# One token-major section of 512 columns in place of two of 256, for the HGRN values and the gMLP's gated half

## The chip, the cores and the metric

The kernel runs on one core of one Trainium2 chip. The metric is the device time of one execution in microseconds (us). A core has a matrix engine (PE, or TensorE), a vector engine (DVE), a scalar engine (ACT), a general engine (POOL), and SP, which here issues DMAs. Products go to eight PSUM banks of 512 float32 columns. PE holds one operand still (the stationary tile, loaded by a weight load, PEld) and moves the columns of the other through it.

## The reference, cut to what matters

One layer of a diffusion backbone on T = 640 tokens: 512 of the sample and 128 of the prompt, each with D = 1024 features. A normalised and modulated h goes through one wide product, whose columns are thirteen sections of 256, and four token mixers use them: a short convolution, a bidirectional HGRN recurrence, a neighbourhood attention and a gMLP. Then follow gates, an output product and a convolutional feed-forward part.

```python
proj = h @ lw['w_in']
(a_x, a_b, a_c, b_q, b_ff, b_fb, b_i, b_g, c_q, c_k, c_v, d_u, d_v) = jnp.split(proj, IN_SPLITS, axis=-1)
...
y_b, s_f, s_b = hgrn2_bidir(b_q, b_ff, b_fb, b_i, b_g, lb_f, lb_b, lw['hgrn_norm_g'], s0_f, s0_b)
...
y_d = chunk_gmlp(d_u, d_v, lw['gmlp_norm_g'], lw['gmlp_ws'], lw['gmlp_b'])
```

The change concerns `b_i`, the values of the recurrence, and `d_v`, the half of the gMLP that is normalised over its 256 features, mixed over 128 tokens and multiplied by `d_u`. All is float32.

## The kernel before, in words

**Products.** To keep float32's accuracy each operand is split into a high part of fewer bits and the low remainder, and a product is three matmuls: high by high, high by low, low by high. The input h lies in SBUF as feature tiles (`xhk`, `xlk`: 128 features by 640 tokens, high and low). A weight arrives by a DMA of 512 KB that SP issues; ACT copies the high part (L311, L324) and DVE subtracts for the low one (L312, L325).

**The input sections.** `SECTIONS` lists the order in which the columns of `w_in` are made. Eleven of the thirteen are *feature-major*: 128 features of the weight are stationary and the tokens move, in two halves of 320 columns (`gemm_half`, L363); a section is two such tiles, each with a weight load of its own. The other two, `i` and `dv`, are *token-major* (`tok_tile`, L917 on): 128 tokens of h are stationary, and the section's 256 weight columns move (L935). For each of the five token tiles there is one accumulation over 8 feature tiles. The weight comes in two steps (`kh`) of 4 feature tiles, and five PSUM banks hold the five sums across both steps. At the second step each token tile is copied out by ACT (L939): the values into the second half of a region HE (tag E), the gated half into DX1 (tag X1). For `dv` ACT also squares it and sums along the row into `dss` (L941), for the normalisation. A `dv` section takes two PSUM pairs of the pool `psg`, of which there are two, and one bank of `psm`, of which there are four; the feature-major tiles take a pair of `psg` each.

**What runs beside them.** The mixers and other work are generators (`hgrn`, `gmlp`, `conva`, `attn`, `ada_cols`, `g_operands`). `start` puts one on a list when a section is done: `hgrn` behind `q`, `gmlp` behind `du`, `conva` behind `ax`, `attn` behind `cv`. The builder keeps an estimated clock. Each product calls `tick(us)` with its estimated time; if a generator's due time has passed, its next piece is issued at that place. A scheduler then sets the order on each engine, where what is marked to stay in program order stays so. The order is thus fixed when the program is built, and each engine works through its own list.

The lines that matter near the changed section:

- `hgrn`: `along` (L467) is a set of two-column matmuls for the recurrence's first level. Then come levels, each with scores on PE (L527, two groups of 40 small matmuls), the selection of them into a tile by DVE (L532, `copy_predicated`), four multiplications that update keys and queries (L546: two for B, two for the tile C), the update of the decays (L550), and copies for the next level's keys (L494 on DVE, L495 on ACT). A level's scores need the C of the level before.
- `ada_cols` (L263): the modulation's products with the condition, as products and row sums on DVE, two of 1024 columns for each of 24 weight rows, with their results at L269; spread over the whole time of the sections.
- `gmlp`: the root of the mean square (L305 on DVE, L306 on POOL), then five scalings of the gated half (L682), then the mixing (L687, L692).
- `attn`: the neighbourhood attention, L829 to L873.

**The loop over units.** Each weight step is a unit of load, split and product. The loop at L1889 issues loads four units ahead and splits two units ahead. Raw weights and split weights have three buffers each.

The order before is `ff fb q i g dv du ck cq cv ac ax ab`; so two feature-major tiles of `g` lie between the two token-major sections. Further on come the gates (L1124, L1137), the output product (L1264), the feed-forward part (L149, L1480, L1815).

Of the kernel before, what the change touches and what calls it, by code (L numbers as in the profile page):

```python
# [12 lines left out]
AF = mybir.ActivationFunctionType  # L13
# [3 lines left out]
P = 128  # L17
# [36 lines left out]

OFF = dict(ax=0, ab=256, ac=512, q=768, ff=1024, fb=1280, i=1536, g=1792,
           cq=2048, ck=2304, cv=2560, du=2816, dv=3072)
SECTIONS = ["ff", "fb", "q", "i", "g", "dv", "du", "ck", "cq", "cv", "ac", "ax", "ab"]


C_C, C_BADA, C_N1, C_N2 = 0, 16, 64, 72  # L60
# [8 lines left out]
def tile_step(ctx: ExitStack, tc: tile.TileContext, a: dict, outs: list, dbg=None):  # L69
# [30 lines left out]
    def tick(us):  # L100
        now[0] += us
        if busy[0]:
            return
        busy[0] = True
        for j in list(jobs):
            if j[0] <= now[0]:
                step(j)
        busy[0] = False
# [19 lines left out]
    def region(tag, shape, dt=F32):  # L128
        return big.tile(shape, dt, tag=tag, name=nm(tag))

    def pm():
        return psm.tile([P, 512], F32, tag="m", name=nm("m"))
# [181 lines left out]
    def feat(src, kt=8, dma=False):  # L314

        raw = rp.tile([P, kt, P], F32, tag="raw", name=nm("raw"))
        nc.sync.dma_start(raw, src)

        def prep(parts=False, tag=None):
            if tag is None:  # L320
                w = wp.tile([P, 2, kt, P], F32R, tag="w", name=nm("w"))
            else:
                w = region(tag, [P, 2, kt, P], F32R)
            high = lambda: act(w[:, 0], raw, AF.Copy)  # L324
            low = lambda: vec.tensor_tensor(w[:, 1], raw, w[:, 0].bitcast(F32), ALU.subtract)  # L325
            if parts:
                return high, low, w
            high()
            if dma:
                low_dma(w[:, 1].rearrange("p a b -> p (a b)"), raw.rearrange("p a b -> p (a b)"))  # L330
            else:
                low()
            return w
        return prep

    def rows(src, nk, nc_, tag=None, dma=False):

        raw = rp.tile([P, nk, nc_], F32, tag="raw", name=nm("raw"))
        nc.sync.dma_start(raw, src)

        def prep():
            if tag is None:
                w = wp.tile([P, 2, nk, nc_], F32R, tag="w", name=nm("w"))
            else:
                w = big.tile([P, 2, nk, nc_], F32R, tag=tag, name=nm("w"))
            if dma:
                act(w[:, 0], raw, AF.Copy)
                low_dma(w[:, 1].rearrange("p a b -> p (a b)"), raw.rearrange("p a b -> p (a b)"))
            else:
                wsplit(raw, (w[:, 0], w[:, 1]))  # L350
            return w
        return prep
# [29 lines left out]
    def need(tag, key, shape, dt=F32):  # L382
        if key not in R:
            R[key] = region(tag, shape, dt)
        return R[key]
# [512 lines left out]
    def plain(ld, cp):  # L898
        units.append((ld, lambda pr: pr(), cp))
# [14 lines left out]
            if sec == "q":  # L914
                start(ada_cols(range(16, 40), "S0", col_home, HD[4], 10), HD[7])

    def tok_tile(sec, kh, w):  # L917

        if kh == 0:
            g0, g1 = pg(), pg()  # L920
            R[sec + "_ps"] = [g0[:, 0, :], g0[:, 1, :], g1[:, 0, :], g1[:, 1, :], pm()]
            if sec == "i":
                dst = need("E", "HE", [P, 2560])[:, 1280:2560]
            else:
                dst = region("X1", [P, 2560])
                R["DX1"] = dst
            R[sec + "_dst"] = dst
        dst = R[sec + "_dst"]
        for t in range(5):
            o = R[sec + "_ps"][t][:, 0:256]  # L930
            for k in range(4):
                ts = slice(t * P, (t + 1) * P)
                kx = kh * 4 + k
                for i, (x, h) in enumerate(((xhk, 0), (xlk, 0), (xhk, 1))):
                    mm(o, x(kx)[:, ts], w[:, h, k, :], start=(kx == 0 and i == 0), stop=(kx == 7 and i == 2))  # L935
                tick(0.33)
            if kh == 1:
                v = dst[:, t * 256:(t + 1) * 256]
                act(v, o, AF.Copy)  # L939
                if sec == "dv":  # L940
                    act(dst[:, 1280 + t * 256:1280 + (t + 1) * 256], v, AF.Square,  # L941
                        accum_out=dss[:, t:t + 1])
        if kh == 1:
            R[sec + "_done"] = True

    TOK = ["i", "dv"]
    for s in SECTIONS:
        for n in range(2):
            if s in TOK:
                plain(lambda s=s, n=n: rows(a["w_tok"][TOK.index(s), n], 4, 256),  # L950
                      lambda w, s=s, n=n: tok_tile(s, n, w))
            else:
                plain(lambda s=s, n=n: feat(a["w_in"][OFF[s] // P + n], dma=s in LOWD),
                      lambda w, s=s, n=n: in_tile(s, n, w))

    hdr = dram.tile([2, 2, P, 4, HC], F32, name="hdr")

# [1171 lines left out]
def host_arrays(inputs):  # L2129

    f = lambda k: np.ascontiguousarray(inputs[k])
    arr = {}
    for k in ["x_prompt", "x_sample", "cache_v", "state_hgrn", "b_ada", "gmlp_b", "final_norm_g"]:
        arr[k] = f(k)

    def tiles(w, k, c):

        return np.ascontiguousarray(w.reshape(k, P, -1, c).transpose(2, 1, 0, 3))

    w_in = f("w_in")[0]  # L2140
    arr["w_in"] = tiles(w_in, 8, P)
    arr["w_tok"] = np.stack([tiles(w_in[:, OFF[s]:OFF[s] + 256], 8, 256)[0].reshape(P, 2, 4, 256)
                             .transpose(1, 0, 2, 3) for s in ("i", "dv")])
    br = np.concatenate([f("w_br_" + b)[0] for b in "abcd"], 1)
    arr["w_gate"] = tiles(np.concatenate([f("w_gate")[0], br], 0), 10, P)

    w = arr["w_gate"].reshape(4, 2, 4, P, 10, P)
    arr["w_gp"] = np.ascontiguousarray(
        np.stack([w[:, 0], w[:, 1][..., [4, 5, 6, 7, 0, 1, 2, 3, 8, 9], :]], 2)).reshape(16, 2, P, 10, P)
    w = tiles(f("w_up")[0], 8, P).reshape(2, NFF, P, 2, 4, P)  # L2150

    arr["w_up"] = np.ascontiguousarray(np.stack([w[0], w[1, :, :, ::-1]], 1))
    w = f("w_ada")[0]
    arr["w_ada"] = tiles(w[:, :2 * D], 8, P)

    arr["w_adt"] = np.ascontiguousarray(w[:, 2 * D:].T.reshape(32, P, D))
    arr["cc"] = np.concatenate([f(k).reshape(1, -1) for k in ("c", "c_ctx")], 0)
    for k in ("w_o", "w_down"):
        w = tiles(f(k)[0], f(k).shape[1] // P, 512)
        arr[k] = np.ascontiguousarray(w.reshape(2, P, -1, 2, 512).transpose(0, 2, 1, 3, 4))  # L2160
    rows = [f(k).reshape(-1, P) for k in ["c", "c_ctx", "b_ada", "norm1_g", "norm2_g", "conv_a_w",
                                          "conv_a_b", "hgrn_lb", "hgrn_norm_g", "gmlp_norm_g", "b_gate"]]
    p1 = np.concatenate(rows, 0).T
    rows = [f(k).reshape(-1, P) for k in ("ffn_conv_w", "ffn_conv_b")]
    arr["p2"] = np.ascontiguousarray(np.concatenate(rows, 0).T)
    arr["gmlp_ws"] = np.ascontiguousarray(f("gmlp_ws")[0].transpose(2, 0, 1).reshape(P, 512))

    arr["cache_k"] = np.ascontiguousarray(f("cache_k")[0, 0].reshape(2, 2, P, 64).transpose(1, 3, 0, 2)
                                          .reshape(P, 256))

    rpb = f("na_rpb")[0]
    pad = np.zeros((4, 15, 64), rpb.dtype)
    pad[:, :, 16:47] = rpb
    r, c = np.arange(8), np.arange(16)
    mgi, ji, ci = np.arange(6), np.arange(8), np.arange(8)
    row = (ji[None, None, None, :, None] - r[:, None, None, None, None] + 7)
    col = (mgi[None, None, :, None, None] * 8 + ci[None, None, None, None, :]
           - c[None, :, None, None, None] - 1 + 16)
    row, col = np.broadcast_arrays(row, col)
    arr["rpbe"] = np.ascontiguousarray(pad[:, row, col].reshape(4, P, 384))  # L2180

    amask = np.zeros((P, 3, 4, 8, 8), np.float32)
    for v in range(3):
        for cc in range(16):
            lo = (max(cc - 8, 0), cc, min(cc + 8, 16))[v]
            for mi in range(32):
                if not (lo <= mi < lo + 16):
                    amask[cc::16, v, mi // 8, :, mi % 8] = -1e30
    arr["amask"] = amask.reshape(P, 768)
    s, t = np.arange(P)[:, None] % 32, np.arange(32)[None, :]  # L2190
    lm = np.zeros((P, 5, 32), np.float32)
    for l in range(5):
        B = 1 << l
        lm[:, l, :] = (s // (2 * B) == t // (2 * B)) & (s // B != t // B)
    arr["lmask"] = lm
    arr["cst"] = np.concatenate([np.eye(P), s == t, p1], 1).astype(np.float32)
    return arr
# [25 lines left out]
```

## Time and profile before

| | us |
|---|---|
| median of 3 runs | 1022.59 (1022.56 to 1022.63) |
| span of the profiled execution | 1020.8 |
| PE busy | 1008.7 |
| DVE busy | 789.7 |
| ACT busy | 538.4 |
| matmuls of L935 | 70.6 to about 123 in the span |

The span goes from the first to the last instruction that the profiler saw in one execution; the median is of the device's own times of other executions of the same program. Matmuls are pipelined: the duration of one (0.28 us at 256 columns) is longer than the spacing to the next, so costs are read from unbroken stretches. In a row of the chain stand the start, the duration, the engine, the tile, the line and how many instructions were joined; "issue" is time for which the profile shows no reason. In a row of the timeline the bracket at the end gives the idle time ahead of the instruction and what ended it.

### The profile page before, as it was taken

The page shows a single profiled execution, that of the slowest core. Times are in us where ns is not written, and L with a number is a line of the kernel's source. Part 1 is how long each engine was busy: PE and PEld are TensorE (multiplying, and loading weights), DVE is VectorE, ACT ScalarE, POOL GpSimd, SP SyncE. Part 2 cuts the span into 40 slices and gives each one's busy share as a digit, 9 for nine tenths or more (in the row PEclk, how much of TensorE's full clock was granted, in tenths as well). Part 3 has the DMA queues.
Part 4 walks back from the last instruction along what each step waited for, and adds up shares of the span by engine and source line. Part 5 has one row for each costly group of instructions (what it writes and reads, how often), then busy time and mean ns, then how long its engine had stood idle before and what let it go on. Part 6 is the DMA issues. An engine that isn't in the chain of part 4 may idle for free.

```text
span 1020.8 us, 18766 instructions
## 1 busy us (share of the span) xinstructions
PE 1008.7 (99%) x7572; PEld 953.0 (93%) x7572; DVE 789.7 (77%) x1308; ACT 538.4 (53%) x933; POOL 106.1 (10%) x153
## 2 busy tenths in 40 slices
PE   8999999999999999999999999999999999999997
PEld 6899999999999999999998899999999999888886
DVE  6759899779857676776868879988888887797644
ACT  6642343354545454444544567777777776633432
POOL 1000020322100000000010111111122211001101
PEclk9999999999999999999999999999999999999999
DMA  9864333697562413323288585755555669974212
GB/s 355 322 217 130 126 117 116 168 284 226 120 207 79 155 58 104 136 66 104 61 283 337 212 325 121 198 151 150 150 151 151 157 161 274 363 249 157 83 42 103
DMA packets 55926, 177.85 MB, mean 174 GB/s; under 512 B 8192, under 2 KB 14624, under 8 KB 53280
## 3 DMA queue, kind: packets, MB, share of 16 engines
q1 hardware_dynamic: 45008, 140.60, 40.2%
q0 software_dynamic: 10832, 36.06, 14.7%
q8 instruction: 59, 0.97, 0.4%
q14 instruction: 27, 0.22, 0.1%
HBM read 134.93 MB, written 25.46 MB: 157 GB/s over the span
## 4 chain that ended last, share of the span: by engine, by line
PE 92%; DVE 4%; DMA 2%; ACT 1%; issue 1%; SPq 0%; POOLq 0%; POOL 0%; DVEq 0%; ACTq 0%
PE g L1480 20%; PE m L1124 17%; PE g L363 14%; PE g L1815 8%; PE m L1815 6%; PE g L1137 5%; PE m L1480 4%; PE m L1264 3%; PE g L935 2%; PE g L1264 2%; PE m L149 2%; PE g L149 1%; PE m L1475 1%; PE m L527 1%; DMA A<-in_w_ada_dram 1%
## 5 line engine op out<-in xcount | busy, mean ns | idle before, releaser
L363 PE MATMUL g<-XH,w 128*128 128x320 f32 x704 | 171.0, 317 | 0.1
L363 PEld LDWEIGHTS g<-XH,w 128*128 128x128 f32 x704 | 120.6, 188 | 2.5 <-issue 1.0
L363 PE MATMUL g<-XL,w 128*128 128x320 f32 x352 | 108.7, 309 | 0.0
L363 PEld LDWEIGHTS g<-XL,w 128*128 128x128 f32 x352 | 66.3, 188 | 0.1
L312 DVE TENSOR_TENSOR w<-raw,w 128x1024 fp32r<-128x1024 f32 x34 | 41.5, 1221 | 14.7 <-ACT w L311 9.0
L1124 PE MATMUL m<-XH,w 128*128 128x320 f32 x224 | 52.5, 309 | 0.0
L1815 PE MATMUL g<-w,XH 128*128 128x512 f32 (+1 forms) x216 | 50.2, 385 | 0.0
L1815 PEld LDWEIGHTS g<-w,XH 128*128 128x128 f32 x216 | 39.5, 188 | 8.3 <-ACT XH L1774 0.3
L311 ACT ACTIVATE w<-raw 128x1024 fp32r<-128x1024 f32 x34 | 35.7, 1049 | 21.4 <-PE g L1264 9.9
L1815 PE MATMUL g<-w,XL 128*128 128x512 f32 (+1 forms) x180 | 42.5, 387 | 0.0
L149 DVE SCALAR_TENSOR_TENSOR X<-MG,p2t,X 128x641 f32<-128x641 f32 x44 | 38.9, 884 | 4.3 <-ACT X L149 3.4
L149 DVE SCALAR_TENSOR_TENSOR X<-X,p2t,X 128x641 f32<-128x641 f32 x44 | 38.8, 883 | 1.9 <-ACT X L149 1.0
L1815 PEld LDWEIGHTS g<-w,XL 128*128 128x128 f32 x180 | 33.4, 188 | 7.4 <-DVE dt L1830 0.7
L149 ACT ACTIVATE w<-raw 128x1024 fp32r<-128x1024 f32 (+3 forms) x46 | 38.5, 852 | 2.5 <-DMA raw<-in_w_in_dram 1.4
L1480 PE MATMUL g<-XL,w 128*128 128x320 f32 x240 | 38.6, 310 | 0.0
L1480 PE MATMUL g<-XL,C 128*128 128x320 f32 x240 | 38.4, 309 | 0.0
L1124 PEld LDWEIGHTS m<-XH,w 128*128 128x128 f32 x224 | 38.2, 188 | 0.0
L1480 PEld LDWEIGHTS g<-XL,w 128*128 128x128 f32 x240 | 36.0, 188 | 0.5 <-ACT MG L149 0.3
L1815 PE MATMUL m<-w,XH 128*128 128x512 f32 (+1 forms) x156 | 36.4, 381 | 0.0
L1480 PEld LDWEIGHTS g<-XL,C 128*128 128x128 f32 x240 | 36.0, 188 | 0.4 <-ACT MG L149 0.4
L1124 PE MATMUL m<-XL,w 128*128 128x320 f32 x112 | 34.6, 309 | 0.0
L1815 PEld LDWEIGHTS m<-w,XH 128*128 128x128 f32 x156 | 28.5, 188 | 5.6
(549 smaller groups left out, 2749.8 us busy)
## 6 DMA issues: line engine op xcount, KB each, us to landing
raw<-in_w_up_dram SPq DMA_DIRECT2D x30, 512.0 KB, 5.0
raw<-in_w_gp_dram SPq DMA_DIRECT2D x21, 640.0 KB, 3.9
raw<-in_w_down_dram SPq DMA_DIRECT2D x22, 512.0 KB, 4.2
raw<-in_w_in_dram SPq DMA_DIRECT2D x19, 512.0 KB, 4.3
H<-in_w_adt_dram SPq DMA_DIRECT2D x16, 512.0 KB, 4.2
actd<-X POOLq DMA_DIRECT2D x22, 320.5 KB, 5.5
X<-in_w_adt_dram SPq DMA_DIRECT2D x10, 512.0 KB, 4.3
upd<-XL SPq DMA_DIRECT2D x4, 1280.0 KB, 6.5
```

Of the source, the lines that this page charges most:

```text
L149: r = f(*args, **kw)
L311: act(w[0], raw, AF.Copy)
L312: vec.tensor_tensor(w[1], raw, w[0].bitcast(F32), ALU.subtract)
L363: mm(o, w[:, h, k0 + k, :], r(k)[:, s], start=(k == 0 and i == 0), stop=(k == kt - 1 and i == 2))
L527: mm(m[W * g:W * g + W, (i - s0) * W:(i - s0 + 1) * W], lhs, rhs, start=True, stop=True, tile_position=(64 * par, W * g))
L935: mm(o, x(kx)[:, ts], w[:, h, k, :], start=(kx == 0 and i == 0), stop=(kx == 7 and i == 2))
L1124: mm(o, w[:, k, :], x[:, k, :], start=(first and k == 0 and j == 0), stop=(k == 3 and j == 2), skip_group_check=True)
L1137: mm(pb[:, c, 0:HC], w[:, h + k, :], y[:, x, k, s], start=(k == 0 and j == 0), stop=(k == 1 and j == 2))
L1264: mm(m, mh[k // 2][:, hx, k % 2, t * P:(t + 1) * P], wo[q][:, hw, k % 2, :], start=(k == 0 and i == 0), stop=(k == 7 and i == 2))
L1475: mm(o, w[:, k, :], x[:, k, :], start=(first and not part and k == 0 and j == 0), stop=(part == 1 and k == 3), skip_group_check=True)
L1480: z = mm(o, w[:, k, :], x[:, k, :], start=(first and k == 0 and j == 0), stop=(k == 3 and j == 2), skip_group_check=True)
L1815: mm(ps, sl[k][hx][:, t * P:(t + 1) * P], w[:, hw, k, c0:c1], start=first, stop=end and (last or nh == 1 and t == 4 and kk_ == 7))
```

## The change

The sections `i` and `dv` become one section `tok`, in the place of `i`, ahead of `g`. Its weight is the columns of both side by side, 512 in all. It comes in four steps (`kq`) of 2 feature tiles, each again 512 KB, and each of the five token tiles has a whole bank. The banks are held over all four steps. In the last step each token tile is evicted by three ACT instructions: the copy of the values, the copy of the gated half, its square with the sum. `tick` is called once for three matmuls with 0.68 (before: 0.33 for three matmuls of half the width). The packing of `w_tok` on the host changes accordingly. In the changed kernel the lines behind L917 move up by 6 at most: the matmul is L931, the evictions L935, L936, L937.

```diff
-SECTIONS = ["ff", "fb", "q", "i", "g", "dv", "du", "ck", "cq", "cv", "ac", "ax", "ab"]
+SECTIONS = ["ff", "fb", "q", "tok", "g", "du", "ck", "cq", "cv", "ac", "ax", "ab"]
...
-    def tok_tile(sec, kh, w):
-
-        if kh == 0:
+    def tok_tile(kq, w):
+
+        if kq == 0:
             g0, g1 = pg(), pg()
-            R[sec + "_ps"] = [g0[:, 0, :], g0[:, 1, :], g1[:, 0, :], g1[:, 1, :], pm()]
-            if sec == "i":
-                dst = need("E", "HE", [P, 2560])[:, 1280:2560]
-            else:
-                dst = region("X1", [P, 2560])
-                R["DX1"] = dst
-            R[sec + "_dst"] = dst
-        dst = R[sec + "_dst"]
+            R["tok_ps"] = [g0[:, 0, :], g0[:, 1, :], g1[:, 0, :], g1[:, 1, :], pm()]
+            need("E", "HE", [P, 2560])
+            R["DX1"] = region("X1", [P, 2560])
+        vi, dv = R["HE"][:, 1280:2560], R["DX1"]
         for t in range(5):
-            o = R[sec + "_ps"][t][:, 0:256]
-            for k in range(4):
-                ts = slice(t * P, (t + 1) * P)
-                kx = kh * 4 + k
+            o = R["tok_ps"][t]
+            ts = slice(t * P, (t + 1) * P)
+            for k in range(2):
+                kx = kq * 2 + k
                 for i, (x, h) in enumerate(((xhk, 0), (xlk, 0), (xhk, 1))):
                     mm(o, x(kx)[:, ts], w[:, h, k, :], start=(kx == 0 and i == 0), stop=(kx == 7 and i == 2))
-                tick(0.33)
-            if kh == 1:
-                v = dst[:, t * 256:(t + 1) * 256]
-                act(v, o, AF.Copy)
-                if sec == "dv":
-                    act(dst[:, 1280 + t * 256:1280 + (t + 1) * 256], v, AF.Square,
-                        accum_out=dss[:, t:t + 1])
-        if kh == 1:
-            R[sec + "_done"] = True
-
-    TOK = ["i", "dv"]
+                tick(0.68)
+            if kq == 3:
+                cs = slice(t * 256, (t + 1) * 256)
+                act(vi[:, cs], o[:, 0:256], AF.Copy)
+                act(dv[:, cs], o[:, 256:512], AF.Copy)
+                act(dv[:, 1280 + t * 256:1280 + (t + 1) * 256], dv[:, cs], AF.Square, accum_out=dss[:, t:t + 1])
+        if kq == 3:
+            R["i_done"] = True
+
     for s in SECTIONS:
+        if s == "tok":
+            for kq in range(4):
+                plain(lambda kq=kq: rows(a["w_tok"][kq], 2, 512), lambda w, kq=kq: tok_tile(kq, w))
+            continue
         for n in range(2):
-            if s in TOK:
-                plain(lambda s=s, n=n: rows(a["w_tok"][TOK.index(s), n], 4, 256),
-                      lambda w, s=s, n=n: tok_tile(s, n, w))
-            else:
-                plain(lambda s=s, n=n: feat(a["w_in"][OFF[s] // P + n], dma=s in LOWD),
-                      lambda w, s=s, n=n: in_tile(s, n, w))
+            plain(lambda s=s, n=n: feat(a["w_in"][OFF[s] // P + n], dma=s in LOWD),
+                  lambda w, s=s, n=n: in_tile(s, n, w))
```

More of the change, by code (lines that the diff above doesn't have):

```diff
@@ L2141, in host_arrays @@
     arr["w_in"] = tiles(w_in, 8, P)
-    arr["w_tok"] = np.stack([tiles(w_in[:, OFF[s]:OFF[s] + 256], 8, 256)[0].reshape(P, 2, 4, 256)
-                             .transpose(1, 0, 2, 3) for s in ("i", "dv")])
+    w = np.concatenate([w_in[:, OFF[s]:OFF[s] + 256] for s in ("i", "dv")], 1)
+    arr["w_tok"] = np.ascontiguousarray(tiles(w, 8, 512)[0].reshape(P, 4, 2, 512).transpose(1, 0, 2, 3))
     br = np.concatenate([f("w_br_" + b)[0] for b in "abcd"], 1)
```

## The prediction

> **What bounds the kernel now.** I read the page first, then the chain of work that ended last, then busy time by windows, then the instructions of PE, DVE and ACT between 60 and 140 us, where the change lies.
>
> ```profile
> span 1020.8 us, 18766 instructions
> PE 1008.7 (99%) x7572; PEld 953.0 (93%) x7572; DVE 789.7 (77%) x1308; ACT 538.4 (53%) x933; POOL 106.1 (10%) x153
> ...
> PE 92%; DVE 4%; DMA 2%; ACT 1%; issue 1%; SPq 0%; POOLq 0%; POOL 0%; DVEq 0%; ACTq 0%
> ```
>
> The third line is the chain: 92% of the span is matmuls that follow one another. So time changes in two ways here: PE gets less to do, or PE stands and waits. DVE is busy for 77% on average, and an average hides stages. So the windows:
>
> ```profile
> 123.00:150.00 27.00, 27.00 (x625) 25.55 (x624) 25.12 (x45) 12.53 (x22) 5.60 (x6) 1.00 0.33 108
> 230.00:260.00 30.00, 29.61 (x238) 27.22 (x237) 29.32 (x72) 14.45 (x34) 8.50 (x11) 1.00 0.76 211
> ```
>
> The columns are length, then PE, weight loads, DVE, ACT and POOL with counts, the granted clock, DMA share and GB/s. In 123 to 150 us PE is full (27.00), and DVE is nearly so: 25.12 of 27. This is just behind the changed section, and DVE there has 1.9 us to spare. The clock stays at 1.00, so it enters no term below.
>
> **What the change removes from PE.** The two sections are 240 matmuls of 256 columns; the new one is 120 of 512. Two rows show the shapes, and chain rows show what an unbroken stretch of each costs.
>
> ```profile
> L935 PE MATMUL g<-w,XH x128: 278/283/387, 70.6 to 120.3; 128*128 128x256 f32 x128
> ```
> ```profile
> L1264 PE MATMUL g<-w,E x24: 389/389/389, 532.6 to 537.8; 128*128 128x512 f32 x24
> ```
> ```profile
> 70.80 5.75 PE g L935 x48
> ...
> 93.63 0.98 PE g L363 x6
> 94.61 0.12 PE m L467 x2
> ...
> 117.64 0.02 issue
> 117.67 0.39 ACT X L939
> 118.06 0.04 issue
> ...
> 126.96 0.82 PE m L527 x58
> 127.78 0.64 PE g L363 x3
> 128.41 0.82 PE m L527 x58
> 129.23 5.48 PE g L363 x36
> ...
> 318.38 1.76 PE g L1137 x12
> ...
> 532.73 5.44 PE g L1264 x24
> ```
>
> Single durations overlap in the pipeline, so I divide stretches: 5.75 / 48 = 0.1198 us at 256 columns, 5.44 / 24 = 0.2267 at 512, 1.76 / 12 = 0.1467 at 320. Before: 240 x 0.1198 = 28.75. After: 120 x 0.2267 = 27.20. **Term 1: -1.55 us.** It is 12.9 ns for each pair made one.
>
> [...]
>
> **The wait that goes.** The chain's 0.02 + 0.39 + 0.04 at 117.64 is PE standing for an eviction of the gated half: its second section took the banks of the running one. The new section holds its five banks once through, and the next product finds one pair of banks to wait for. I leave 0.15-0.2 of such a wait. **Term 2: -0.28** (bounds -0.45 and 0).
>
> **What is moved.** Loads (four of 512 KB), their splitting on ACT and DVE, and the 15 eviction operations keep number and size; I count them at nothing as work. The small state products between the wide matmuls keep their number too (18 groups in the section, 14 against 13 behind it). Such a group costs 0.98 + 0.12 - 6 x 0.1467 = 0.22 us in both. What moves is order. All gated-half evictions now come before g, some 20 us earlier, so the gMLP's normalisation (the square root at L305/L306, five products at L682) is released earlier, and the instruction order puts it on DVE between the recurrence's levels 1 and 2. Before, it came behind level 4:
>
> ```profile
> 116.24 1.35 DVE L550 TENSOR_TENSOR A<-A 128x640 f32<-128x640 f32 x1
> ...
> 124.20 0.81 DVE L550 TENSOR_TENSOR A<-A 128x320 f32<-128x320 f32 x1
> 124.92 1.22 DVE L263 SCALAR_TENSOR_TENSOR junk<-X,S 128x1024 bf16<-128x1024 f32 x1
> ...
> 126.06 1.22 DVE L325 TENSOR_TENSOR w<-raw,w 128x1024 fp32r<-128x1024 f32 x1
> 127.20 1.21 DVE L263 SCALAR_TENSOR_TENSOR X<-X,S 128x1024 f32<-128x1024 f32 x1
> ...
> 128.34 0.81 DVE L546 TENSOR_TENSOR B<-B,A 128x640 f32<-128x640 f32 x1
> 129.08 0.22 DVE L269 TENSOR_SCALAR gcol<-ar,cst 128x2 f32<-128x2 f32 x1
> 129.21 0.51 DVE L532 COPY_PREDICATED D<-lmask,m 128x320 f32<-128x320 uint8 x1
> 129.61 0.81 DVE L546 TENSOR_TENSOR B<-B,A 128x640 f32<-128x640 f32 x1
> 130.34 0.48 DVE L494 COPY E<-B 128x640 f32<-128x640 f32 x1
> 130.75 0.52 DVE L532 COPY_PREDICATED D<-lmask,m 128x320 f32<-128x320 uint8 x1
> 131.15 1.54 DVE L546 TENSOR_TENSOR C<-C,A 128x640 f32<-128x640 f32 x2
> ...
> 132.97 0.16 DVE L305 TENSOR_SCALAR dss<-dss 128x5 f32<-128x5 f32 x1
> ...
> 135.00 0.62 DVE L682 TENSOR_SCALAR X<-X,dss 128x256 f32<-128x256 f32 x2 [0.33 <-POOL dss L306]
> 135.53 1.22 DVE L325 TENSOR_TENSOR w<-raw,w 128x1024 fp32r<-128x1024 f32 x1
> ```
> ```profile
> 133.21 1.75 POOL L306 TENSOR_TENSOR dss<-dss,neghalf 128x5 f32<-128x5 f32 x1 [81.87 <-DVE dss L305]
> ```
> ```profile
> 87.89 1.05 ACT L311 ACTIVATE w<-raw 128x1024 fp32r<-128x1024 f32 x1
> ...
> 117.67 0.38 ACT L939 ACTIVATE X<-g 128x256 f32<-128x256 f32 x1
> 118.08 0.42 ACT L941 ACTIVATE X<-X 128x256 f32<-128x256 f32 x1
> 118.41 0.18 ACT L941 ACTIVATION_READ_ACCUMULATOR X<-X 128x1 f32 x1
> ```
>
> From start to start, a L263 or L325 takes 1.14 us, a L546 0.73, L532 0.40, L494 0.41, L269 0.13, L682 about 0.27; L550 takes 1.26 on 640 columns and 0.72 on 320. The scores of a level (PE, L527) need the two L546 that make C. So the question is whether DVE has C before PE arrives.
>
> PE in the new order. The section starts at 70.7 and takes 27.2 + 18 x 0.22 = 31.2, with the start-up some 0.3 more: it ends at 102.2. Then 33 matmuls of g (33 x 0.1467 = 4.84) and level 1 at 107.05. A level period is 0.82 + 0.64 + 0.82 + 5.48 = 7.76, so PE arrives for level 2 at 114.8, level 3 at 122.6, level 4 at 130.3 if nothing holds it.
>
> DVE in the new order. A weight's low part (L325) waits for an ACT copy that now stands behind the last tile's three evictions: 102.2 + 1.7 (copy, copy, square and its accumulator: 0.38 + 0.38 + 0.42 + 0.18, and 0.3 of release) + 1.0 = 104.9. Then L325 1.14, L263 1.14, L305 at about 107.2. The first L682 comes 135.00 - 132.97 = 2.03 after that, at 109.2, with a L263 in the gap. Then L682, L269, L532, four L682, L532 and two L546: 0.27 + 0.13 + 0.40 + 1.06 + 0.40 + 1.47 = 3.73, so level 2's C is ready at 113.0. That is 1.8 before PE: **no wait at level 2.** Behind it a level on DVE is longer than before, since the condition's products (L263) are bunched: three of them and a L325 to a level, where the level quoted above has two and a L325. Level 3: L550 1.26 + 4 x 1.14 + L546 4 x 0.73 + L269 0.13 + L532 2 x 0.40 + L494 0.41 = 10.1; level 4 with a L550 of 0.72: 9.6. Before, the quoted level took 132.62 - 124.20 = 8.4, which is 9.6 less one L263. So level 3's C is ready at 123.1, PE waits 0.5; level 4's at 132.7, and PE, delayed to 130.9, waits 1.8. Behind level 4 DVE's list is shorter, as five L682 (1.3 us) and the 2 us of L305 and POOL are done; it is ahead again at level 5 (139.4 against 142.7). **Term 3: +2.3 us.** The bounds, from the same sum with DVE 2 us earlier or later: 0 and +4.3. I take +2.3, since each duration in it is a row.
>
> [...]
>
> **The rest.** POOL's order is the same. SP issues the same loads in a slightly changed order; the first of the section's loads are split well ahead. In attention (the second window, DVE 29.32 of 30) DVE has equal work in both orders, but PE's saved time would make it wait there if DVE were not equally early; bounds 0 and +2, taken 0, since from 70 to 230 DVE has slack enough to follow. After 283 us the instruction orders are the same.
>
> **Sum.** -1.55 - 0.28 + 2.3 = +0.47 us on the profiled execution. Its span is 1020.8, the median of the runs 1022.59, so 1.8 lies around the span, which I keep: 1020.8 + 0.5 + 1.8 = **1023.1 us**.
>
> **The rivals.**
> *The wide matmuls pay and nothing waits (1020.8).* Condition: DVE reaches level 4's C 2.3 us earlier than in my sum. For it: DVE's rows before show L263 filling any gap, and if the condition's products run earlier, while PE is in the wide section, the levels are shorter. Against: the order is fixed when the program is built, and I read it. -1.55 - 0.28 = -1.83 gives 1020.8.
>
> *DVE falls behind for good (1026).* The slower side. The place is the one L325 behind the evictions and the L305/L306/L682 sequence. If it lies 2 us later than in my sum (ACT held up by its other work, 12.53 busy of 27 in the window, or POOL late), level 2's C comes after 114.8, and from that point on each us later is a us of PE waiting: +2 at the levels, and about 1 in attention, where DVE has nothing to spare: 1023.1 + 3 = 1026.
>
> *The change doesn't do what it says (1024.6).* A 512-column matmul in this place, with the token tiles as the stationary side, costs twice 0.1198. Then term 1 is nothing: 1023.1 + 1.55 = 1024.65. [...] Against: the quoted L1264 stretch, also with a new stationary tile for each matmul.
>
> **How the numbers follow.** Chances: forecast 0.50 (1021.3 to 1024.6, from DVE a little early or late), no waits 0.27, DVE behind 0.20, no saving 0.03. The range 1020.4 to 1026.2 takes in the best of the no-wait case (another 0.4 us less) and the slower case. A measurement of this kernel tells about 0.2%, or 2.05 us, from no change: 1020.54 and 1024.64. Half of the no-wait case lies under the first: 0.15 faster. The slower case, half of the last and some of the forecast lie over the second: 0.25. The rest, 0.60, is the same.
>
> **What would show it.** Term 1: a stretch of 48 wide matmuls without small ones between them takes 10.9 us. Term 2: no ACT wait of 0.4 in front of the section's successors. Term 3: the L682 lie between levels 1 and 2 on DVE, and L527 has idle time released by DVE C L546 at two levels, 0.5 and 1.8 us, between 120 and 134. If these waits are absent, the time is near 1020.8; if they are over 4, term 3's start, 104.9 for the weight behind the evictions, was wrong. New PE waits after 230 us would make attention the cause.

## The result and the profile after

The changed kernel takes 1030.85 us (median of 4, 1030.26 to 1032.48) against 1022.61 for the kernel before: ratio 1.0083, 95% interval 1.0071 to 1.0096, so 8.2 us slower. The forecast was 1023.1 with a range from 1020.4 to 1026.2, so the time lies outside the range. Of all executions in this document one, of e11, ran at a granted clock of 0.556 and took 1649.92 us; it is left out of what follows.

The page of the changed kernel, the same three lines as were shown of before:

```profile
span 1028.4 us, 18526 instructions
PE 1009.8 (98%) x7452; PEld 947.7 (92%) x7452; DVE 789.1 (77%) x1308; ACT 537.4 (52%) x933; POOL 110.1 (11%) x153
...
PE 77%; DVE 8%; issue 7%; DMA 3%; ACT 2%; POOL 1%; SPq 0%; POOLq 0%; DVEq 0%; ACTq 0%
```

PE has 120 matmuls fewer (7452 against 7572) and yet 1.1 us more busy time, and the chain is no longer nearly all PE. The waits of PE between 60 and 300 us in the changed kernel (engine, tile, line, what it waited for; then us, times, the longest):

```profile
PE m L527 <- issue: 1.8, 1, 1.8
PE m L649 <- DVE MG L653: 1.5, 1, 1.5
PE m L849 <- DVE C L873: 1.1, 1, 1.1
PE m L527 <- DVE C L546: 0.8, 1, 0.8
PE m L849 <- DVE X L846: 0.4, 1, 0.4
PE m L866 <- ACT B L1925: 0.3, 1, 0.3
```

Before, this list had one line, 0.4 at L849. The same view's timeline at level 3 of the recurrence, PE alone:

```profile
123.28 0.31 PE L363 MATMUL g<-XH,w 128*128 128x320 f32 x1
124.37 0.88 PE L527 MATMUL m<-C,D 64*32 64x32 f32 x80 [0.78 <-DVE C L546]
...
125.82 0.38 PE L527 MATMUL m<-C,D 64*32 64x32 f32 x20
127.98 0.71 PE L527 MATMUL m<-C,D 64*32 64x32 f32 x60 [1.78 <-issue]
```

PE first stands 0.78 us for DVE's C. Then it stops again inside a group of 80 small matmuls that had already begun, behind the 20th, for 1.78 us, and the bracket names no engine; the records of the other 60 hold no wait for a semaphore, so nothing that DVE or ACT does is on record as its cause. What follows is slower too. Windows of the changed kernel (length, PE, weight loads, DVE, ACT, POOL, granted clock, DMA share, GB/s):

```profile
121.90:125.30 3.40, 2.62 (x93) 2.35 (x92) 3.40 (x6) 2.28 (x3) 0.00 (x0) 1.00 0.08 34
125.30:128.70 3.40, 1.61 (x84) 1.27 (x84) 3.40 (x7) 0.00 (x0) 0.00 (x0) 1.00 0.49 137
128.70:132.10 3.40, 3.40 (x13) 3.40 (x14) 3.40 (x7) 0.15 (x1) 0.00 (x0) 0.51 0.76 205
132.10:135.50 3.40, 3.40 (x24) 3.34 (x23) 3.40 (x7) 1.23 (x3) 0.00 (x0) 0.99 0.32 130
```

In the third window the granted clock is 0.51: 13 matmuls in 3.4 us, where the next window has 24. In the chain the stretch between this level and the next is

```profile
128.70 7.00 PE g L363 x36
```

against 5.48 for the same 36 before: 1.5 us lost to the clock. DVE is busy in all four windows without a gap (3.40 of 3.40).

**Where the 7.6 us of the two spans lie.** For every matmul I took the distance to the next one's start less any standing, and summed by line:

| part | before | after | difference, us |
|---|---|---|---|
| matmuls of the token-major section(s) | 30.66 | 29.15 | -1.51 |
| matmuls of L363 (half clock for 3.41 us) | 177.34 | 179.40 | +2.06 |
| standing at level 3 (C, then "issue") | 0 | 0.78 + 1.78 | +2.56 |
| standing at L649 | 0 | 1.55 | +1.55 |
| standing in attention (L849, L866) | 0.39 | 1.80 | +1.41 |
| three lines of attention's matmuls, interleaved otherwise | 12.07 | 12.74 | +0.67 |
| standing at L1809 near 944 us, on the landing of a 1 MB DMA | 0 | 0.78 | +0.78 |

Together +7.5 of 7.6. The saving of the first row is there, and the other rows outweigh it.

### The profile page after: what moved, and what is told of

It is laid out like the page before. It is cut to its first block, busy times and chain, and to the rows that moved or that the text cites. A ratio compares the mean times of both kernels' runs of the same rounds, so it can differ in the third digit from the quotient of the medians.

```text
span 1028.4 us, 18526 instructions
## 1 busy us (share of the span) xinstructions
PE 1009.8 (98%) x7452; PEld 947.7 (92%) x7452; DVE 789.1 (77%) x1308; ACT 537.4 (52%) x933; POOL 110.1 (11%) x153
## 4 chain that ended last, share of the span: by engine, by line
PE 77%; DVE 8%; issue 7%; DMA 3%; ACT 2%; POOL 1%; SPq 0%; POOLq 0%; DVEq 0%; ACTq 0%
PE g L1474 19%; PE m L1118 17%; PE g L1809 8%; PE g L363 8%; PE m L1809 5%; PE g L1131 5%; PE m L1474 4%; PE m L1258 3%; PE g L1258 2%; PE m L149 1%; DVE junk L263 1%; PE m L1469 1%; DMA A<-in_w_ada_dram 1%; PE g L149 1%; POOL hss L306 1%
## 5 line engine op out<-in xcount | busy, mean ns | idle before, releaser
L363 PE MATMUL g<-XH,w 128*128 128x320 f32 x704 | 170.2, 318 | 0.1
L363 PEld LDWEIGHTS g<-XH,w 128*128 128x128 f32 x704 | 121.1, 190 | 2.9 <-issue 1.0
L363 PE MATMUL g<-XL,w 128*128 128x320 f32 x352 | 109.9, 312 | 0.0
L363 PEld LDWEIGHTS g<-XL,w 128*128 128x128 f32 x352 | 66.9, 190 | 0.0
L1809 PE MATMUL g<-w,XH 128*128 128x512 f32 (+1 forms) x216 | 50.2, 385 | 0.0
L1809 PEld LDWEIGHTS g<-w,XH 128*128 128x128 f32 x216 | 39.5, 188 | 8.2 <-ACT XH L1768 0.3
L1809 PE MATMUL g<-w,XL 128*128 128x512 f32 (+1 forms) x180 | 42.5, 386 | 0.8 <-DVE dt L1824 0.8
L1809 PEld LDWEIGHTS g<-w,XL 128*128 128x128 f32 x180 | 33.4, 188 | 8.1 <-DVE dt L1824 1.4
L1809 PE MATMUL m<-w,XH 128*128 128x512 f32 (+1 forms) x156 | 36.4, 381 | 0.0
L1809 PEld LDWEIGHTS m<-w,XH 128*128 128x128 f32 x156 | 28.5, 188 | 5.6
```

Source lines behind the costliest of these rows:

```text
L363: mm(o, w[:, h, k0 + k, :], r(k)[:, s], start=(k == 0 and i == 0), stop=(k == kt - 1 and i == 2))
L1809: mm(ps, sl[k][hx][:, t * P:(t + 1) * P], w[:, hw, k, c0:c1], start=first, stop=end and (last or nh == 1 and t == 4 and kk_ == 7))
```

## The experiments

**Theory A**: PE's loss begins where DVE is late by the new order of its list. A stop of PE costs more than itself: it holds back the fetch of PE's own code (the "issue" of 1.78), and with too little work the clock goes to half behind it (0.51 from 128.70 to 132.10). **Rivals**: B, the second stop too is a wait for DVE; C, the position of the code blocks alone makes it, whatever DVE does; D, the wide matmuls or the banks held for four steps cost it. C and D were tried by runs of their own (e2 and e9; e3, e4 and e7).

Each profile is of one execution of its run. In e7 that one took 1032.46 us where the median is 1027.41, in e5 1029.54 where it is 1027.56, in e6 1028.93 where it is 1027.01: the waits listed there explain the profiled execution, and the median only in part.

The DMA records of the trace have a queue of kind "instruction" (q8). In the changed kernel it moves 58 blocks of 16384 bytes, one for 258 on average of the 14993 recorded PE instructions (matmuls, weight loads, semaphore instructions), so I take it for PE's code. One of them starts at 125.38 and takes 1.21 us, so it ends within the stop (126.20 to 127.98). PE stops when exactly 2753 of its instructions have started.

### e8: the changed kernel again

> The changed kernel again, unaltered, for a second profile. Theory A: what is fixed by the order comes again: the wait for C at level 3 (0.8), the code stop in its second group behind PE instruction 2753 (1.8), the half clock behind it, L649 1.5, L849 1 to 2. What was chance in the first profile goes (0.78 us at L1809 near 944). About 1030.9.

Measured: 1031.60 (1029.28 to 1033.17), 1.0082 [1.0065, 1.0099]. The stops came again: 0.75 for C, 1.72 behind instruction 2753, half clock for 3.41 us, 1.59 at L649, 1.71 at L849. So did 0.82 at L1809, which I had called chance. There the 1 MB load that DVE waits for takes 5.7 and 5.8 us from issue to landing in the two profiles, 5.1 before and 4.7 in e2, where PE didn't wait. In all 17 profiles of this case it takes 5.7 to 6.6 in the five where PE waited (the change, e8, and with 1.56, 1.03 and 1.56 e5, e9 and e12), and 4.2 to 5.2 in the others, where PE stood 0.16 at most. All five have the change's order, but e1, e2, e3 and e10 have it too and did not wait. Whether the order makes a long load likelier is not shown. The other rows of the table came again, that at L849 larger than the first time (1.07).

### e1: 50 PE instructions more in front

```diff
-                    mm(o, x(kx)[:, ts], w[:, h, k, :], start=(kx == 0 and i == 0), stop=(kx == 7 and i == 2))
+                    for lo, hi in ((0, 256), (256, 512)) if (kx or i) and kq == 0 else ((0, 512),):
+                        mm(o[:, lo:hi], x(kx)[:, ts], w[:, h, k, lo:hi], start=(kx == 0 and i == 0),
+                           stop=(kx == 7 and i == 2 and hi == 512))
```

> The changed kernel, with 25 of its 120 matmuls of 512 columns (all of the first step but each bank's first) written as two of 256. That adds 25 weight loads and 25 matmuls, 50 PE instructions, at 25 x 12.9 ns = 0.3 us, and moves every later block of PE's code by 50 instructions against the work; the order on DVE at levels 2 to 5 stays. Theory A (the 1.78 us at 126.20 is PE waiting for a block of its own instructions, whose fetch could not be asked for while PE stood at level 3's wait; the half clock behind it follows from the standing): with the block's edge 50 instructions earlier the fetch is asked for before the wait, the 1.78 goes, the half clock (1.7) goes, the wait of 0.8 for C stays: 1030.9 + 0.3 - 3.5 = 1027.7. Theory B (the 1.78 belongs to the late C and DVE): the stop stays, 1031.2.

Measured: 1028.78 (1028.04 to 1029.69), 1.0059 [1.0044, 1.0074]. At level 3 there is no stop, as expected, but there is one at level 2, which I had not expected:

```profile
118.05 0.77 PE L527 MATMUL m<-C,E 64*32 64x32 f32 x67
120.35 0.32 PE L527 MATMUL m<-C,E 64*32 64x32 f32 x13 [1.53 <-issue]
```

PE stops behind instruction 2497, which is 2753 - 256. The work moved by 50 instructions and the stop went to another edge of the same grid. With that the stop is tied to a count of PE's instructions and not to a piece of work; rival B falls, since at level 2 PE waits for no C. But theory A does not cover this stop either, as no wait of PE goes ahead of it. The wait for C at level 3, which I had expected to stay, went: delayed at level 2, PE came to level 3 at 127.6, with C done at 125.0.

### e3: all of the section in narrow matmuls

The same edit with the condition `(kx or i)` alone: 115 pairs.

> The changed kernel's order and its one section, but all matmuls (but each bank's first) as two of 256 columns. Width theory (12.9 ns a pair): the section itself is 1.5 us longer, 1032.3 if the stop stays. The 230 more PE instructions are one block of 256 less 26, so by theory A the block's edge lies 26 instructions later against the work and the stop at level 3 is still there. If the width is worth nothing, the time stays at 1030.9.

Measured: 1031.66 (1028.50 to 1032.13), 1.0077 [1.0058, 1.0095]. The stop is there (1.73 at level 3), behind instruction 3009 = 2753 + 256. The section's matmuls take 30.16, 1.01 more than wide. Its median is 0.8 above that of the change, within the spread of both; the width is worth at most its 1 to 1.5 us, and it isn't what costs.

### e2: the normalisation kept behind the levels

```diff
-        rstd(ss[:, 0:5], ss[:, 0:5], 5, 1.0 / 256)
+        tc.keep_in_program_order(vec.tensor_scalar(ss[:, 0:5], ss[:, 0:5], 1.0 / 256, EPS, ALU.mult, ALU.add))
+        pool.tensor_tensor(ss[:, 0:5], ss[:, 0:5], neghalf[:, 0:5], ALU.pow)
...
-            vec.tensor_scalar(v, v, ss[:, t:t + 1], None, ALU.mult)
+            tc.keep_in_program_order(vec.tensor_scalar(v, v, ss[:, t:t + 1], None, ALU.mult))
```

> The changed kernel, with L305 and the five L682 kept in the program's order on DVE: they then stand behind level 5 instead of ahead of level 2's C. Nothing else moves on DVE up to there. DVE gains about 1.06 (its wait for POOL) and 1.4 of work ahead of level 2, so level 3's C is ready near 122 and PE comes at 123.5. Theory A: no wait at level 3, so PE's sequencer is not held, the fetch comes in time, no half clock: 1030.9 - 0.8 - 1.8 - 1.7 = 1026.6. Theory C (position of the code block alone makes the 1.78 stop, whatever DVE does): only 0.8 goes, 1029 to 1030. The waits from 200 us on (L649, L849) stay in both.

Measured: 1029.48 (1028.20 to 1030.51), 1.0065 [1.0050, 1.0080]. Level 3 came out as theory A has it: no wait for C, and the stop behind 2753, at the same instruction as in the change, is 0.50 in place of 1.78, with no half clock there. So the position of the block alone (rival C) does not make the 1.78.

```profile
124.96 0.38 PE L527 MATMUL m<-C,D 64*32 64x32 f32 x20
125.84 0.71 PE L527 MATMUL m<-C,D 64*32 64x32 f32 x60 [0.50 <-issue]
```

The fetch starts at 123.52 and not at 125.38, 1.16 us behind the end of C in both. But the total fell by 1.4 and not by 4: the normalisation now holds DVE at about 150 us (two waits of 0.4 at L527), PE stands 2.07 at L649, and the half clock comes there, from 202.04. The delay was moved.

### e9: the normalisation's scalings on ACT

```diff
-            vec.tensor_scalar(v, v, ss[:, t:t + 1], None, ALU.mult)
+            act(v, v, AF.Copy, scale=ss[:, t:t + 1])
```

> The changed kernel, with the five scalings of the gated half (L682) on ACT in place of DVE; the lists of DVE and PE are otherwise as they were. DVE loses the wait for POOL (1.06) and 1.4 of work ahead of level 2's C, so C of level 3 is ready near 122, before PE comes at 123.5. Theory A: the wait of 0.8 goes, the code stop shrinks to 0 to 0.5 since PE's sequencer isn't held, the half clock goes: 1030.9 - 0.8 - 1.5 - 1.6 = 1027. The waits from 200 us on stay. Theory C (block position alone): 1029 to 1030.

Measured: 1027.17 (1025.49 to 1027.59), 1.0038 [1.0023, 1.0053]. That is within 0.2 of what was expected, but by luck, as the parts below differ. PE's waits in it from 60 to 300 us:

```profile
PE m L649 <- DVE MG L653: 1.6, 1, 1.6
PE m L849 <- DVE C L873: 1.1, 1, 1.1
PE g L363 <- issue: 1.1, 1, 1.1
PE m L849 <- DVE X L846: 0.4, 1, 0.4
PE m L866 <- ACT B L1925: 0.3, 1, 0.3
```

The wait for C and the half clock are gone, and so is the stop behind 2753. A code stop of 1.05 came instead at an earlier edge (behind 2497), and 1.03 at L1809. Why the block for that edge came late here, with C early, these runs don't show.

### e7: only the order, with the old width

```diff
-SECTIONS = ["ff", "fb", "q", "i", "g", "dv", "du", "ck", "cq", "cv", "ac", "ax", "ab"]
+SECTIONS = ["ff", "fb", "q", "i", "dv", "g", "du", "ck", "cq", "cv", "ac", "ax", "ab"]
```

> The kernel before, with only the order of its sections changed to q, i, dv, g, du: two sections of 256 columns as they were, one behind the other. Order theory: the gated half's evictions come early as in the changed kernel, the normalisation stands ahead of level 2, L263 ahead of L653, and the time is the changed kernel's and 1.5 us for the narrow matmuls: 1030 to 1032.5. Width theory (the wide matmuls, or banks held for all four steps, are what costs): near 1022.6.

Measured: 1027.41 (1025.31 to 1032.46), 1.0039 [1.0024, 1.0055]. Slower than before without a wide matmul; the sum that I had expected (1030 or more) was too large for the median, though its profiled execution, with a span of 1030.6, has it. Its waits:

```profile
PE m L866 <- DVE B L1933: 2.6, 1, 2.6
PE m L527 <- issue: 1.7, 1, 1.7
PE m L649 <- DVE MG L653: 1.1, 1, 1.1
```

The stop at level 3 is behind instruction 3009. Rival D is out as the main cause: the order alone makes waits of the same kind, though not all at the same places (none for C at L527, none at L849). PE came to level 3 at 124.7, 0.2 after C was done, so here the code stop came without PE having stood for C. The windows around the wait of 2.6 show the clock once more:

```profile
235.30:238.70 3.40, 1.31 (x9) 1.05 (x8) 3.40 (x9) 1.69 (x5) 1.42 (x2) 1.00 0.41 164
238.70:245.50 6.80, 6.33 (x30) 5.32 (x31) 4.33 (x12) 2.22 (x6) 2.29 (x3) 0.50 0.65 154
245.50:248.90 3.40, 3.40 (x27) 3.40 (x26) 2.98 (x6) 2.53 (x5) 0.00 (x0) 0.99 0.85 265
```

### e10 and e11: DVE relieved by leaving work out

```diff
-                    vec.scalar_tensor_tensor(raw if v else junk, raw, 1.0, cr[:, v], ALU.mult, ALU.mult,
+                    vec.scalar_tensor_tensor((raw if v else junk)[:, 0:512], raw[:, 0:512], 1.0, cr[:, v, 0:512], ALU.mult, ALU.mult,
```

> The changed kernel with the condition's products (L263) over 512 of their 1024 columns: half of that sum is left out, so that about 26 us of DVE's work between 70 and 240 us are gone. Theory (everything above the width's gain is PE waiting for a late DVE and what follows from that): all waits at L527, L649 and L849 but that for X of 0.4 go, and the kernel is 1.5 us faster than the kernel before treated alike: 1020.5 to 1021. Rival (the loss is PE's own: code blocks, more changes between shapes): it stays 4 us or more above.

> The kernel before with the same half of the condition's sums left out. It had next to no waits for DVE (0.4 at L849), so both theories expect 1022.2 to 1022.6.

Measured: the changed kernel 1020.28 (1019.73 to 1021.79; ratio to the kernel before 0.9974 [0.9964, 0.9984]), the kernel before 1021.60 (1021.44 to 1022.91; 0.9990 [0.9980, 0.9999]). With DVE relieved the change is 1.3 us faster, the size of term 1. (The profiled executions differ by 0.3 only: that of the changed kernel is the slowest of its ten, and still stands 1.3 in attention. The kernel before came out 0.6 below what I had expected; its wait of 0.39 at L849 is gone, and attention's matmuls take 11.68 in place of 12.07, which I had not counted.) PE's waits in the changed kernel so treated:

```profile
PE m L849 <- DVE C L873: 1.0, 1, 1.0
PE m L866 <- ACT B L1925: 0.3, 1, 0.3
```

All waits at the levels and at L649 are gone, and those in attention are not, though I had expected them to go.

### e5, e4 and e6: the order by two other handles

e5 is the change with `tick(0.66)`. e4 has the sections in the order `"q", "g", "tok", "du"`. e6 has both.

> The changed kernel with tick(0.66) in place of 0.68, so that the new section moves the builder's clock by 26.4 as the two old ones did (2 x 40 x 0.33). No instruction is added or taken away; in DVE's list the L263 that stood ahead of the first L653 now stands elsewhere, as before the change. Theory A with order: the 1.55 us wait at L649 goes and the rest (C at level 3, the code stop, the half clock) stays, since the lists up to there are nearly the same: 1030.9 - 1.6 = 1029.3. If the clock's total were the cause of all waits, it is near 1022.

Measured: 1027.56 (1026.32 to 1029.54), 1.0049 [1.0036, 1.0063].

```profile
PE m L849 <- DVE C L873: 1.9, 1, 1.9
PE m L527 <- DVE C L546: 1.7, 1, 1.7
```

The wait at L649 is gone, as expected: with the product L263 out of the way of L653, PE does not wait there. At level 3 there is neither wait nor stop, where I had expected both to stay. Then level 4 has a wait of 1.71, the size and place that the prediction had named. Both waits listed are followed by a half clock of 3.41 us.

> The wide section in the place of the old gated half: q, g, tok, du. The gMLP's normalisation then stands behind level 4 on DVE again. If the order of DVE's work at the levels is what costs (theories A and B), no wait at levels 2 to 4, and the saving of 1.55 shows: 1021 to 1022. If the width or the banks held over four steps cost, it is over 1023. Waits from 200 us on may differ, as the order there changes too.

Measured: 1024.03 (1023.63 to 1024.70), 1.0013 [1.0004, 1.0022]. The levels wait for nothing, attention neither; what is left is 0.44 of the wide section standing for one of its own evictions (L936), 0.20, and 1.43 at L649. The section's matmuls gain 1.10. So the expectation for the levels held, and 1021 to 1022 did not, by the wait at L649. The time is over the 1023 that I had set as a sign of the width or the held banks, but of these only the 0.44 shows.

> q, g, tok, du with tick(0.66). DVE's list has no extra product ahead of L653, so the 1.43 wait at L649 of the run with g first goes: 1024.0 - 1.4 = 1022.6, which is level with before. If the width's 1.5 us is to be had as well, other waits of that run must have hidden it, and it is 1021 to 1021.5.

Measured: 1027.01 (1026.68 to 1028.93), 1.0046 [1.0033, 1.0058]. A miss: L649's wait went, and attention got one of 3.20 at L866, with 6.83 us of half clock. A change of 0.02 in an estimate moves the waits about; none of these lists was made with them in view.

### e12 to e15: DVE relieved with all work done

```diff
-LOWD = ("ac", "ax", "ab", "d")
+LOWD = ("g", "du", "ck", "cq", "cv", "ac", "ax", "ab", "d")
```

> The changed kernel, with the low part of ten weights (g, du, ck, cq, cv) made as the sections ac, ax and ab do it already (ACT writes the negated high part, a DMA issued by POOL adds the weight to it), not by DVE. That takes 10 x 1.14 = 11.4 us from DVE between 95 and 220 us and leaves nothing out. Theory A: no wait at levels 2 to 5, no half clock there; the waits at L649 (an extra L263 ahead of L653 is still in the list) and in attention (eight steps L708/L710 in one pair, order as in the changed kernel) stay, if they hang on the order; then 1030.9 - 4.2 = 1026 to 1027. If they only hang on DVE's backlog, they go too, and it is 1021.

Measured: 1025.69 (1024.76 to 1026.87), 1.0030 [1.0018, 1.0041].

```profile
PE m L849 <- DVE C L873: 1.3, 1, 1.3
PE g L363 <- issue: 1.3, 1, 1.3
PE m L849 <- DVE X L846: 0.4, 1, 0.4
PE m L866 <- ACT B L1925: 0.3, 1, 0.3
```

No wait at the levels, no half clock; and L649's wait went too, though L263 still stands ahead of L653. So that one hung on the backlog, and I was wrong to count on the list there. Attention's waits stay, and so do its matmuls' +0.67: they come with the order. The stop of 1.29 for code lies behind 2497, as in e9, and 1.56 at L1809 comes on top.

> The same relief with the wide section behind g (q, g, tok, du). DVE's list in attention is that of the kernel before, word for word in its first 60 entries. Theory A: no waits at the levels or in attention, that at L649 shrinks; the width's gain of 1.1 to 1.5 shows: 1021.0 to 1022.0 against 1022.5 of before. Rival (width gains nothing in a complete kernel): 1022.5 or more.

> The kernel before with the same ten weights relieved. It waits for DVE only at L849 (0.4) and for an eviction, so the relief should give at most 0.4: 1022.2 to 1022.7.

Measured: e13 1022.52 (1021.77 to 1024.94), 1.0000 [0.9991, 1.0008]; e14, the kernel before so relieved, 1022.92 (1022.04 to 1024.01), 1.0002 [0.9993, 1.0011]. PE's waits in e13 from 60 to 300 us:

```profile
PE m L849 <- DVE X L846: 0.5, 1, 0.5
PE g L931 <- ACT X L936: 0.4, 1, 0.4
PE m L649 <- DVE MG L653: 0.2, 1, 0.2
```

With the section behind g, which gives attention its old order, and DVE relieved, the change costs nothing any more. Its section gains 1.13 and loses 0.45 at an eviction, and the median is the rival's 1022.5, above the 1022.0 that I had expected at most: a gain over before can't be told from none (0.4 against e14, inside the intervals). In e14 PE's one wait there is a code stop of 0.41, behind 2753.

> q, g, tok, du with only the five L682 on ACT. It had 1024.0 without that, with 1.43 at L649. L682 lies at 138 us and DVE has idle time between there and 200, so theory A expects little: 1023.5 to 1024.

Measured: 1023.63 (1023.15 to 1024.12), 1.0008 [0.9999, 1.0018], as expected. The wait at L649 is 1.43 in it too: DVE's scalings at 138 us have nothing to do with that one.

No version here that does all the work beats the kernel before by more than a measurement tells. The width could bring 1.5 us at most, 0.15%.

## Why the prediction was wrong

Two terms of the sum failed: term 3, in which a wait of PE costs its own length, and "the rest", which was put at nothing.

- **Term 1, -1.55: right.** The section's matmuls went from 30.66 to 29.15, -1.51 or 12.6 ns a pair, and e10 against e11 agrees with it in the times (-1.3).
- **Term 2, -0.28: a misreading.** PE did not stand for the 0.45 us that the chain of the kernel before gives to the eviction. Its timeline shows small matmuls of the levels in that time, so that at most 0.1 us was to be had (118.01 to 118.10):

```profile
117.56 0.45 PE L527 MATMUL m<-C,E 64*32 64x32 f32 x30
118.10 0.38 PE L935 MATMUL g<-w,XH 128*128 128x256 f32 x1
```

- **DVE's list and level 2: right.** The normalisation stands between levels 1 and 2. The changed kernel's DVE rows:

```profile
110.34 0.35 DVE L682 TENSOR_SCALAR X<-X,dss 128x256 f32<-128x256 f32 x1 [1.06 <-POOL dss L306]
...
112.59 1.55 DVE L546 TENSOR_TENSOR C<-C,A 128x640 f32<-128x640 f32 x2
...
122.67 1.55 DVE L546 TENSOR_TENSOR C<-C,A 128x640 f32<-128x640 f32 x2
```

  C for level 2 is done at 114.1 (forecast 113.0) and PE needs it at 115.8 (114.8): no wait. C for level 3 is done at 124.2 (123.1), PE is there at 123.6 (122.6): a wait of 0.78 where 0.5 was forecast. Both sides are 1 us late, since the section ends at 103.1 and not at 102.2.
- **Term 3, +2.3: the step that failed is the price of a wait.** I took a wait of PE to cost its own length. At level 3 a wait of 0.78 was followed by 1.78 for code and by 3.41 us at half clock, 1.5 of them lost: some 4.1 us. The sum had no term for either. e7 adds a code stop of 1.69 without a wait of PE, where C was done 0.2 us before PE came. The wait of 1.8 forecast for level 4 did not come in the change, because PE was by then, at 135.6, 4.7 us later than the sum had it (130.9), and C was done at 133.7; in e5, without the stop at level 3, it came with 1.71.
- **"The rest", taken at 0: failed.** I took DVE's work as equal in both orders and its slack from 70 to 230 us as enough. It measured 1.55 at L649 and 2.1 in attention, and 0.78 at L1809 of open origin. What counts is which instruction stands in front of which at the time, and how late DVE is there. The changed kernel at 201 us:

```profile
201.06 1.22 DVE L263 SCALAR_TENSOR_TENSOR junk<-A,S 128x1024 bf16<-128x1024 f32 x1
...
202.32 0.61 DVE L653 SCALAR_TENSOR_TENSOR MG<-m,cst,MG 128x128 f32<-128x128 f32 x2
```
```profile
202.72 0.33 PE L649 MATMUL m<-cst,MG 128*128 128x128 f32 x1 [1.55 <-DVE MG L653]
```

  One product of 1.14 us ahead of L653, on a DVE that is already behind, is 1.55 us of PE (e5 and e12 take it away in two ways). In attention the new interleaving costs 1.4 of standing and 0.7 of matmuls, in e12 still, in e13 no more. Why it costs that is not taken apart by these runs.
- **The rival "DVE falls behind for good"** had the direction right, with 3 us beyond the forecast where 7.7 were needed. Its condition, level 2's C later than PE, did not come (114.1 against 115.8). That attention would pay for a late DVE was in it with "about 1".
- **The clock "enters no term"** was said from a profile in which PE hardly ever stood. In the kernel before it is 1.00 over all of 60 to 1000 us, with PE busy for 938.73 of 940. The change made PE stand, and behind the 1.78 at level 3 it is 0.51.

What stays open: why the block at 2497 came late in e1, e9 and e12; what the small matmuls count for when the clock is set (last section); and the long load at L1809.

## What to carry to other kernels

On an engine that is full, look beyond the length of a new wait, at what its own code fetch and its clock do when it stands: here a wait of 0.78 us was followed by a stop of 1.78 and by 1.5 lost at half clock. Equal work on the neighbour is no argument; go through its list and see what stands ahead of each instruction that the full engine needs. Here the wider matmuls gave 1.51 us, 0.15%, and the other rows of the table cost 9.0, so try the order by itself first.

## What the runs showed of the hardware

**Code blocks.** In the change 58 blocks of 16384 bytes come for 14993 recorded PE instructions. Eight stops of 0.5 to 1.78 us in eight profiles lie behind instruction 2497 (e1, e9, e12), 2753 (the change, e8, e2) or 3009 (e3, e7), all 256 apart. Two shorter ones, in versions of the kernel before, lie on the same grid: 0.25 behind 2241 (e11) and 0.41 behind 2753 (e14). PE goes on 2.2 to 2.7 us after the block's DMA has started (2.60 in the change, 2.32 in e2, 2.71 in e1, 2.21 in e14). In seven profiles (the change, e8, e2, e3, e7, e9, e10) a fetch starts 1.06 to 1.30 us behind the end of level 3's C, 1.16 in the change; that PE asks for the block only once C is there is my inference, and no record shows it. What goes with the length of the stop is how long after C's end PE reaches the edge: 1.97 to 2.10 us in the change, e8, e3 and e7, which stopped 1.69 to 1.78; 2.98 in e2, which stopped 0.50; 3.76 and 3.99 in e10 and e9, which did not stop there. The stops of e1, e9, e12, e11 and e14 have no wait of PE ahead of them, so a wait is not the only way to a late block.

A group of 80 small matmuls uses 160 instructions in 0.8 us, and two groups with three wide matmuls between them are more than a block in 2.3 us; 36 matmuls of 320 columns use 72 in 5.5. So where the small matmuls stand, a block can be used up in less time than the 2.2 to 2.7 us.

**The clock.** Between 60 and 1000 us the clock went to half (0.5 in the trace's clock record) for 3.41 us, or twice that, after PE had stood 1.78 (the change, 0.78 ahead of it), 1.72 (e8), 1.53 (e1), 2.07 (e2), 1.73 (e3), 1.71 and 1.94 (e5), 3.20 (e6), 1.69 and 2.56 (e7). It did not after 1.55 to 1.59 at L649 (the change, e1, e3, e8, e9), nor after 1.71 to 1.74 at L849 (e1, e8, e2), nor 2.38 at L849 (e3). The starts lie on a grid of 3.413 us from the beginning of the record (36 steps in the change, 34 in e1, 57 in e2). Cut along that grid, the cases come apart. The 2.38 of e3 falls into two windows, with 1.10 and 1.28. In windows without small matmuls of the levels the clock stayed with up to 1.74 us of standing (e2) and went with 1.94 or more (e5). In windows with them 1.53 was enough (e1), and 0.78 was not (the change). From these cases I infer that the work within one window decides, and that a small matmul counts for less than its time; neither is shown beyond them, and for how much it counts isn't settled.
